# A decoder trunk on one core: combination tiles claimed early, gate chunks stored in pairs, the last three gate units kept on chip, weight units fetched a block ahead

## The chip, the cores and the metric

The kernel runs on one core of a Trainium2 chip. That core has a matrix engine (TensorE, PE in the profile, with a separate sequencer for the weight loads, PEld), a vector engine (VectorE, DVE), an activation engine (ScalarE, ACT), a general engine (GpSimd, POOL) and a queue engine (SyncE, SP), from which nearly all of this kernel's DMA transfers are issued. The metric is the device time of one execution, in microseconds; lower is better.

## The reference, cut to what matters

One layer of a decoder trunk is applied to 1024 prompt positions and to 8 samples of 4 new positions each, 1056 columns in all, at a model width of 1024. The middle part, which the change touches, is the mixing step between two feed-forward halves:

```
z = h @ w_in + b_in                         # q, k, v, uv, gate A, gate B
outs, lses = attention of 3 head groups (window, dilation) = (128,1), (512,4), (2048,16)
w   = softmax(lses over the 3 groups)       # one weight per head and position
att = sum over groups of outs * w           # "combination", 256 wide
yb  = u * (tril(W_s) @ LN(v) + b)           # gMLP branch, 512 wide
mix = (sigmoid(gA) * (att @ w_oa) + sigmoid(gB) * (yb @ w_ob)) @ w_out
h   = LN2(alpha * h + mix)
```

The prompt and the samples share all weights. The samples also attend to a cache of keys and values. Gate A and gate B are 1024 wide each, that is eight blocks of 128 rows each.

## The kernel before, in words

**Layout.** Activations lie transposed: 128 features on the partitions and 1056 columns (`NT`; the prompt alone is `NP` = 1024) along the free axis. The columns are worked in four chunks of `C` = 264. All products are in fp32r as three passes, high by high, high by low and low by high (`mm3`, L240), so that a weight and an activation are first split into a high and a low part (`split`, L251 on ACT and L252 on DVE).

**Pools.** `S` has 37 slots of a full row block (1056 columns), `W` 8 tiles for split weights, `M` 6 tiles of medium size, `R` and `Q` 2 each for raw data, and PSUM has 3 `mm` and 5 `ax` buffers. A tile takes the buffer of an older one when that one's last reader is done. `held` (L105 to L109) takes a slot and at once writes one column of it on POOL, so that the slot belongs to it from then on; without the write, the first real write claims it.

**Order of the work.** The program is written as generators in three queues (`bg`, `slow`, `mid`); `tick` steps them between two pieces of dense work. The Tile framework then schedules each engine's instructions by a simulated timeline, and a tag "urgent" draws an instruction forward. What an engine executes is therefore a fixed row of instructions, in the scheduler's order, and an engine waits at the first one that is not ready.

**The mixing stage.** `mix` (L1524) runs from about 1064 us to 1400 us of the profile.

- *Plain gate units.* Ten units (6 to 15 of the gate list, `NLEAD` = 6, `NTAIL` = 10) are dense products: one 128-wide block of `w_in` against eight blocks of `h`. `gate8` (L984 to L992) does one chunk: 24 matmuls into an `mm` buffer, an eviction on ACT into an `M` tile (L990), a store of the 132 KB chunk to the scratch array `zD` (L991), and a `tick`. Units 6 to 12 run all four chunks in the order 0, 2, 1, 3. Units 13 to 15 (`LAST` = 3) are fetched together and run chunks 0 to 2; their last chunk is run much later (`beside`), next to the output products.
- *Attention.* `attend(i)` runs six times, for the two head pairs and three groups (attend 0 to 2 are head pair 0, attend 3 to 5 head pair 1). Each has four steps of scores (L1200 on PE, bias and minimum L1208 on DVE, exponential L1212 on ACT), of turning the probabilities (L1223 on PE, copy L1227 on ACT) and of values (L1239 on PE, copy L1246 or L1250 on ACT), and at the end a transpose of the row minima and sums (L1261) that are stored to `mlD` (L1265). The dense chunks stand between the steps.
- *Combination.* After group 2 of a head pair, `combine(hp)` (L1272 to L1328) loads the minima and sums back (L1283 to L1289), computes the weights on DVE and ACT (L1297 to L1310), stores them to `cD` (L1312), fetches them broadcast over 64 partitions (L1319) and multiplies and adds on DVE (L1324, L1326, L1327). Its tiles are `raw`, `att` and three `cbs`; the last four are taken after the stores.
- *Samples.* The cached keys and values are loaded in pieces (`M<-kv`) and worked on DVE (L1392, L1397, L1398).
- *Output products.* `local(n)` multiplies gate B block n by `yb @ w_ob` (the product's eviction is the multiplication L1541 on DVE). The gate blocks `mt` are fetched from `zD` (L1138), and a narrow weight unit `wo` is fetched at the head of each block (`narrow`, L225 to L234). After the last `att` is split, the same is done for gate A (`ta`, fetched at L1580), block by block, with the late chunks of the units 13 to 15 beside blocks 2, 4 and 5. The sum of both is split for the last product, `w_out`.

## Time and profile before

| | us |
|---|---|
| median of 3 runs | 2202.6 (2198.51 to 2202.74) |
| profiled execution, device time | 2202.1 |
| its span in the trace | 2200.3 |
| busy in the span: PE, DVE, ACT, POOL | 2132.7, 1555.3, 892.8, 321.6 |
| mixing stage, 1064 to 1400 us: span and PE busy | 336.0 and 298.64 |

A row of the page names a line and engine, the operation, what it writes and reads by the program's names, how often it occurs, its total and mean time, and the idle time of that engine just before it with what ended the idle time. A timeline row has its start, its length, the engine, the line and operation, how many neighbouring instructions it sums up, and in brackets the idle time before it. In the windows table each engine has its busy time in that stretch and then the clock that PE was granted (1.00 is full).

### The profile page before, as it was taken

How to read it: one execution, taken by the hardware profiler on the slowest of the kernel's cores; microseconds unless marked ns; L12 is line 12 of the kernel's file. 1: busy time of each engine (PE TensorE's matmuls, PEld its weight loads, DVE VectorE, ACT ScalarE, POOL GpSimd, SP SyncE). 2: the span in 40 equal slices, each digit the busy share in tenths (PEclk: the TensorE clock that was granted, in tenths of full speed). 3: DMA queues.
4: the chain of work that ended last, by engine and by line, in shares of the span. 5: the costliest groups of instructions: out<-in, count | busy, mean ns of one | idle time of the engine just before them, and what ended most of it. 6: DMA issues, size and time to landing. Idle time of an engine off the chain costs nothing.

```text
span 2200.3 us, 43275 instructions
## 1 busy us (share of the span) xinstructions
PE 2132.7 (97%) x17305; PEld 2093.7 (95%) x17305; DVE 1555.3 (71%) x2724; ACT 892.8 (41%) x1681; POOL 321.6 (15%) x234
## 2 busy tenths in 40 slices
PE   9999999999998999999989988999999999999997
PEld 8999999999998999999879877999999999999997
DVE  8776776656788726787674647778576777656887
ACT  5444444421225634344465453245344444421224
POOL 0432332200010022232000000000332233100000
PEclk9999999999999999999999998999999999999998
DMA  4435545598973325666854637514354454597841
GB/s 157 146 134 178 176 161 175 194 372 319 329 279 134 136 101 193 205 219 222 312 166 151 186 119 244 195 41 143 129 185 156 166 185 159 181 393 290 303 183 79
DMA packets 170553, 429.01 MB, mean 195 GB/s; under 512 B 24864, under 2 KB 61584, under 8 KB 167664
## 3 DMA queue, kind: packets, MB, share of 16 engines
q1 hardware_dynamic: 169920, 425.71, 55.1%
q8 instruction: 135, 2.21, 0.4%
q14 instruction: 66, 0.54, 0.1%
q10 hardware_dynamic: 432, 0.54, 0.1%
HBM read 305.56 MB, written 166.81 MB: 215 GB/s over the span
## 4 chain that ended last, share of the span: by engine, by line
PE 83%; DMA 7%; DVE 6%; ACT 2%; issue 1%; SPq 1%; POOL 0%; ACTq 0%; DVEq 0%; POOLq 0%
PE ax L240 44%; PE mm L240 35%; DMA M<-kv 3%; DMA zD<-M 1%; DVE W L252 1%; PE ax L1200 1%; DMA S<-zD 1%; DVE X L1382 1%; PE ax L1223 1%; DVE S L252 1%; PE ax L1239 0%; DVE M L1392 0%; DVE S L627 0%; DVE M L1381 0%; DVE X L1397 0%
## 5 line engine op out<-in xcount | busy, mean ns | idle before, releaser
L240 PE MATMUL mm<-S,W 128*128 128x264 f32 x5208 | 694.8, 289 | 30.1 <-DVE S L1541 13.2
L240 PE MATMUL ax<-S,W 128*128 128x264 f32 x5400 | 706.9, 284 | 0.4 <-DVE W L252 0.2
L240 PEld LDWEIGHTS mm<-S,W 128*128 128x128 f32 x5208 | 659.2, 191 | 46.8 <-DVE S L1541 15.2
L240 PEld LDWEIGHTS ax<-S,W 128*128 128x128 f32 x5400 | 677.0, 188 | 2.7 <-ACT S L1030 0.8
L240 PE MATMUL ax<-S,S 128*128 128x264 f32 x3240 | 478.7, 285 | 4.0 <-DVE S L1039 3.9
L240 PEld LDWEIGHTS ax<-S,S 128*128 128x128 f32 x3240 | 429.6, 189 | 5.3 <-DVE S L1039 5.3
L240 PE MATMUL mm<-S,S 128*128 128x264 f32 x2472 | 383.8, 285 | 2.6 <-DVE S L252 2.0
L240 PEld LDWEIGHTS mm<-S,S 128*128 128x128 f32 x2472 | 333.7, 188 | 4.3 <-DVE S L252 2.2
L251 ACT CAST W<-R 128x1024 fp32r<-128x1024 f32 (+3 forms) x173 | 128.8, 761 | 319.7 <-PE mm L240 137.4
L382 POOL TENSOR_TENSOR Q<-R 128x512 f32<-128x512 f32 x49 | 70.3, 1434 | 798.2 <-DMA R<-w13a 202.8
L252 DVE TENSOR_TENSOR W<-R,W 128x1024 fp32r<-128x1024 f32 (+3 forms) x173 | 152.1, 883 | 26.7 <-ACT W L251 22.2
L251 ACT CAST W<-Q 128x1024 fp32r<-128x1024 f32 (+1 forms) x78 | 76.8, 984 | 224.2 <-POOL Q L383 89.4
L816 DVE SCALAR_TENSOR_TENSOR S<-ax,S 128x264 f32<-128x264 f32 x240 | 99.4, 427 | 66.8 <-PE ax L240 65.7
L457 DVE TENSOR_TENSOR S<-ax,M 128x264 f32<-128x264 f32 x82 | 32.8, 432 | 151.3 <-PE ax L240 151.3
L108 POOL CAST S<-ones 128x1 fp32r<-128x1 f32 x32 | 17.6, 571 | 751.4 <-DVE S L1633 363.5
L252 DVE TENSOR_TENSOR S<-Q,S 128x1024 fp32r<-128x1024 f32 (+1 forms) x78 | 112.6, 1444 | 3.8 <-ACT S L251 3.8
L252 DVE TENSOR_TENSOR W<-Q,W 128x1024 fp32r<-128x1024 f32 (+1 forms) x78 | 89.6, 1149 | 26.6 <-ACT W L251 26.6
L251 ACT CAST S<-Q 128x1024 fp32r<-128x1024 f32 (+1 forms) x78 | 76.8, 984 | 68.1 <-PE ax L240 49.7
L251 ACT CAST S<-R 128x512 fp32r<-128x512 f32 (+1 forms) x64 | 44.1, 689 | 105.9 <-DMA sumsA<-S 39.4
L252 DVE TENSOR_TENSOR S<-S,M 128x528 fp32r<-128x528 f32 x72 | 84.5, 1174 | 2.6 <-ACT M L251 0.8
L383 POOL TENSOR_TENSOR Q<-Q,R 128x512 f32<-128x512 f32 x49 | 81.0, 1653 | 2.7
L390 POOL TENSOR_TENSOR Q<-R,Q 128x512 f32<-128x512 f32 x49 | 80.5, 1644 | 1.1
(204 smaller groups left out, 2049.6 us busy)
## 6 DMA issues: line engine op xcount, KB each, us to landing
ws<-st SPq DMA_DIRECT2D x144, 256.0 KB
S<-sumsA SPq DMA_DIRECT2D x63, 528.0 KB
S<-sumsB SPq DMA_DIRECT2D x63, 528.0 KB
M<-kv SPq DMA_DIRECT2D x96, 256.0 KB
sumsA<-M SPq DMA_DIRECT2D x90, 264.0 KB
sumsB<-M SPq DMA_DIRECT2D x90, 264.0 KB
R<-w13b SPq DMA_DIRECT2D x44, 512.0 KB
R<-w13a SPq DMA_DIRECT2D x42, 512.0 KB
```

The lines of the kernel that those rows point to most:

```text
L108: self.nc.gpsimd.tensor_copy(t[:, 0, :1] if len(shape) == 3 else t[:, :1], self.ones[:, :1])
L240: mm = lambda a, b, s, e: nc.tensor.matmul(o, a[:, cc], b, start=s, stop=e, skip_group_check=True)
L251: a = self.nc.scalar.copy(hi, src)
L252: b = self.nc.vector.tensor_tensor(lo, src, hi.bitcast(F32), op=ALU.subtract)
L382: tt(s12[:, lo], cd[:, lo], cd[:, hi], op=ALU.add)
L383: tt(s12[:, hi], s12[:, lo], ab[:, lo], op=ALU.subtract)
L390: tt(s34[:, hi], ab[:, hi], s12[:, hi], op=ALU.subtract)
L457: go(one, 5, False, lambda x: tt(h[:, x, 1], one[x], p7[:, x], op=ALU.add))
L816: nc.vector.scalar_tensor_tensor(y(x, r, e), bank[x], HALF, y(x, r, e), op0=ALU.mult, op1=ALU.add)
L1200: nc.tensor.matmul(pS[h][:, r, :nk], q[e, i * P : (i + 1) * P], k[e, k0 : k0 + nk], start=True, stop=True)
L1223: nc.tensor.transpose(pT[r][:, h, o], s[:, r, h, o], self.ident)
L1382: nc.vector.tensor_reduce(o, t, axis=AX.X, op=ALU.add)
```

## The change

**Combination.** `combine` takes `raw`, `att` and the three `cbs` at its start, all five with `held`, so a one-column write on POOL claims each. Nothing else of its computation changes, but each `cb` is now a full-width slot of which `NP` columns are used.

**Plain gate units 6 to 12.** Each unit is fetched while the one before it is worked. The chunks 0 and 2 go into the two halves of one `W` tile, the chunks 1 and 3 into another (the last of these units uses `M` tiles), each pair with one store instead of two: 14 stores in place of 28.

**Units 13 to 15.** They are evicted straight into held slots (`kept`), chunk by chunk, and are neither stored to `zD` nor fetched back: 9 stores and 3 fetches go. The three units are fetched while unit 12 is worked, and the three slots are claimed then.

**Narrow units.** `wo` units are fetched one block ahead in both loops of output products.

Line numbers of the new program differ by a few from here on: L1585 is the eviction of a chunk pair, L1587 its store, L1569 the eviction of a kept unit, L1314 the store to `cD`.

```diff
@@ -1272,7 +1272,9 @@
     def combine(self, hp):
         nc = self.nc
         t = []
-        raw = self.S([16, 3, 2, P])
+        slot = self.held
+        raw = slot([P, 3 * 2 * P])[:16].rearrange("p (g m x) -> p g m x", g=3, m=2)
+        att, *cbs = [slot([P, NT]) for _ in range(4)]
         for g in range(3):
             x = raw[:, g]
             for m in range(2):
@@ -1311,15 +1313,13 @@
         for g in range(3):
             nc.sync.dma_start(self.cD[hp, g].rearrange("h (a x) -> (h a) x", a=8), t[g][:, 1])
         yield
-        att = self.S([P, NT])
         self.att[hp] = att
-        cbs = [self.S([P, NP]) for _ in range(3)]
         for g, cb in enumerate(cbs):
             for h in range(2):
-                nc.sync.dma_start(cb[64 * h : 64 * h + 64], self.cD[hp, g, h].partition_broadcast(64))
+                nc.sync.dma_start(cb[64 * h : 64 * h + 64, :NP], self.cD[hp, g, h].partition_broadcast(64))
         yield from self.pause(3)
         for g, cb in enumerate(cbs):
-            aT = self.attT.pop((hp, g))
+            cb, aT = cb[:, :NP], self.attT.pop((hp, g))
             if g == 0:
                 nc.vector.tensor_tensor(att[:, :NP], aT, cb, op=ALU.mult)
             else:
@@ -1541,7 +1541,9 @@
                 nc.vector.tensor_tensor(t[:, cc], t[:, cc], p, op=ALU.mult)
 
         def local(n):
-            wb = self.narrow(a["wo"][n, :, 2 * P :], 4 * P)
+            wb = wbs.popleft()
+            if n + 1 < KB:
+                wbs.append(self.narrow(a["wo"][n + 1, :, 2 * P :], 4 * P))
             if n + 6 < KB:
                 with self.tc.high_priority(offset=URGENT):
                     mt[n + 6] = self.fetch_z(40 + n)
@@ -1557,11 +1559,34 @@
         sgu = [self.sgu_norm()] + [self.sgu_mix(gg) for gg in range(4)]
         self.mid.extend(sgu)
         self.bg.extend(self.attend(i) for i in range(len(HPG)))
-        for n in range(NLEAD, NLEAD + NTAIL - LAST):
-            w = self.unit(a["wzp"][n])
-            for c in (0, 2, 1, 3):
-                self.gate8(w, DENSE[n], c, AF.Identity, STEPS["tail"], 1)
-        units = {n: self.unit(a["wzp"][n]) for n in range(NLEAD + NTAIL - LAST, NLEAD + NTAIL)}
+        kept, end = {}, NLEAD + NTAIL - LAST
+        units = {NLEAD: self.unit(a["wzp"][NLEAD])}
+
+        def gate(n, c, *steps):
+            p = self.mm_tile()[:, :C]
+            self.dense8(p, units[n], c)
+            with self.urgent():
+                nc.scalar.activation(kept[n][:, c * C : c * C + C], p, AF.Identity, bias=self.bin(DENSE[n]))
+            self.tick(*steps)
+
+        for n in range(NLEAD, end):
+            w = units.pop(n)
+            for m in range(n + 1, n + 2 if n + 1 < end else NLEAD + NTAIL):
+                units[m] = self.unit(a["wzp"][m])
+                if m >= end:
+                    kept[m] = self.held([P, NT])
+            z = self.zD[DENSE[n]].rearrange("p (a b x) -> p b a x", a=2, b=2)
+            for b in range(2):
+                t = (self.W if n + 1 < end else self.M)([P, 2, C], F32)
+                for x in range(2):
+                    p = self.mm_tile()[:, :C]
+                    self.dense8(p, w, 2 * x + b)
+                    with self.urgent():
+                        nc.scalar.activation(t[:, x], p, AF.Identity, bias=self.bin(DENSE[n]))
+                    if x:
+                        nc.sync.dma_start(z[:, b], t)
+                    self.tick(STEPS["tail"], 1)
+        w = None
         for c in range(NC):
             if c:
                 with self.tc.high_priority(offset=URGENT):
@@ -1569,23 +1594,9 @@
                         mt[n] = self.fetch_z(34 + n)
             if c < NC - 1:
                 for n in units:
-                    self.gate8(units[n], DENSE[n], c, AF.Identity, STEPS["tail"], 1)
+                    gate(n, c, STEPS["tail"], 1)
         while any(g in self.mid for g in sgu):
             self.step(self.mid, 1)
-
-        def fetch_gate(n):
-            held = 26 + n in [DENSE[m] for m in units]
-            t = self.S([P, NT])
-            cc = slice(0, (NC - 1) * C if held else NT)
-            nc.sync.dma_start(t[:, cc], self.zD[26 + n][:, cc])
-            return t
-
-        def beside(n):
-            m = DENSE[n] - 26
-            p = self.mm_tile()[:, :C]
-            self.dense8(p, units.pop(n), NC - 1)
-            with self.urgent():
-                nc.scalar.activation(ta[m][:, -C:], p, AF.Identity, bias=self.bin(DENSE[n]))
 
         def column_sums():
             wr, wsum = self.X([P, KB - half, KB], "wr", 1), self.X([P, KB], "wsum", 1)
@@ -1612,19 +1623,24 @@
         done, half = 0, 3
         sums = column_sums()
         self.slow.append(sums)
+        wbs = deque([self.narrow(a["wo"][0, :, 2 * P :], 4 * P)])
         for n in range(KB):
             local(n)
+        was = deque([self.narrow(a["wo"][0, :, : 2 * P], 2 * P)])
         self.yb = None
-        ta = [fetch_gate(n) for n in range(3)]
+        ta = [self.fetch_z(26 + n) for n in range(3)]
         while self.bg or self.mid or self.slow[0] is not sums:
             self.tick(1, 1 if self.slow[0] is not sums else 0)
         split_att()
 
         m2 = []
         for n in range(KB):
-            wa = self.narrow(a["wo"][n, :, : 2 * P], 2 * P)
+            wa = was.popleft()
+            if n + 1 < KB:
+                was.append(self.narrow(a["wo"][n + 1, :, : 2 * P], 2 * P))
             if n + 3 < KB:
-                ta.append(fetch_gate(n + 3))
+                m = NLEAD + NTAIL - KB + n + 3
+                ta.append(kept[m] if m in kept else self.fetch_z(29 + n))
             if 26 + n in LATE_GATES:
                 nc.scalar.activation(ta[n], ta[n], AF.Sigmoid)
             for c in range(NC):
@@ -1635,8 +1651,8 @@
             self.split(*m2[n], mt[n])
             done += 1
             if n in BESIDE:
-                beside(BESIDE[n])
-        units = self.A = None
+                gate(BESIDE[n], NC - 1, 0, 0)
+        units = kept = self.A = None
         self.sqs, self.lns = {}, {}
         self.Y = self.new_Y(self.hD[0])
 
```

How this moves the work on the engines is seen best at three places. Names have the letter of the pool and a number; `mm` and `ax` are PSUM buffers.

ScalarE around attend 3 (head pair 1, group 0), before: between the exponentials (L1212) and copies (L1227) of this attention stand evictions of gate chunks (L990).

```order
L990 ACTIVATE M_14702<-mm_14677,cols 128x264
L1212 ACTIVATE S_14316,X_14256<-S_14316,X_14256 128x256
L1212 ACTIVATE S_14316,X_14256<-S_14316,X_14256 128x256
L990 ACTIVATE M_14789<-mm_14764,cols 128x264
L1212 ACTIVATE S_14316,X_14256<-S_14316,X_14256 128x256 x2
L990 ACTIVATE M_14873<-mm_14848,cols 128x264
L1227 COPY S_14348<-ax_14339 128x512
L1227 COPY S_14348<-ax_14338 128x512
L990 ACTIVATE M_14913<-mm_14888,cols 128x264
L1212 ACTIVATE S_14351,X_14256<-S_14351,X_14256 128x256 x4
```

The same place of ScalarE after the change:

```order
L1227 COPY S_14338<-ax_14328 128x512
L1227 COPY S_14338<-ax_14329 128x512
L1212 ACTIVATE S_14341,X_14247<-S_14341,X_14247 128x256 x2
L1246 COPY S_14248<-ax_14321 128x512
L1212 ACTIVATE S_14341,X_14247<-S_14341,X_14247 128x256 x2
L1227 COPY S_14409<-ax_14399 128x512
L1227 COPY S_14409<-ax_14400 128x512
L1212 ACTIVATE S_14412,X_14247<-S_14412,X_14247 128x256 x4
L1227 COPY S_14476<-ax_14466 128x512
L1227 COPY S_14476<-ax_14467 128x512
L1569 ACTIVATE S_14498<-mm_14747,cols 128x264
L1569 ACTIVATE S_14507<-mm_14829,cols 128x264
```

The three first chunks of the kept units (`mm_14747`, `mm_14829`, `mm_14867`), whose matmuls stand on PE ahead of all of attend 3's turns, are evicted behind its last copies, each after its claim on POOL. There are three `mm` buffers, so no dense chunk stands on PE between these turns any more.

SyncE at the end of attend 5, before: the stores of the combination's weights and their fetches stand ahead of four fetches of gate blocks.

```order
L1312 DMA cD<-S_15274 16x128
L1312 DMA cD<-S_15274 16x128
L1319 DMA S_15307<-cD 64x1024
L1319 DMA S_15307<-cD 64x1024
L1319 DMA S_15308<-cD 64x1024
L1319 DMA S_15308<-cD 64x1024
L1319 DMA S_15309<-cD 64x1024
L1138 DMA S_15316<-zD_8666 128x1056
L1138 DMA S_15318<-zD_8667 128x1056
L1138 DMA S_15326<-zD_8668 128x1056
L1138 DMA S_15413<-zD_8669 128x1056
L1319 DMA S_15309<-cD 64x1024
```

The same four fetches of SyncE after the change, with the rows about them:

```order
L1138 DMA S_15118<-zD_8664 128x1056
L1138 DMA S_15120<-zD_8665 128x1056
L1285 DMA S_15239<-mlD 8x128
L1138 DMA S_15286<-zD_8666 128x1056
L1138 DMA S_15288<-zD_8667 128x1056
L1138 DMA S_15302<-zD_8668 128x1056
L1138 DMA S_15389<-zD_8669 128x1056
L1265 DMA mlD<-X_15200 32x128
L1285 DMA S_15239<-mlD 8x128
```

The fetches of `zD_8666` to `zD_8669` have moved ahead of the store of attend 5's minima and sums (L1265), and so ahead of the whole combination of head pair 1.

VectorE at the second combination, before: the multiplication L1324 stands ahead of four blocks of products (L1541 is the eviction of one chunk of a product).

```order
L1308 RECIPROCAL X_15287<-X_15287 16x128
L1310 TENSOR_TENSOR S_15274<-X_15287,S_15274 16x128 x3
L1324 TENSOR_TENSOR S_15306<-S_14257,S_15307 128x1024
L1326 TENSOR_TENSOR S_14630<-S_14630,S_15308 128x1024
L1434 COPY S_15306<-ax_15636 64x32 x2
L1541 TENSOR_TENSOR S_15316<-S_15316,mm_15622 128x264
```

The same place of VectorE after the change:

```order
L1312 TENSOR_TENSOR S_15239<-X_15261,S_15239 16x128 x3
L1607 TENSOR_REDUCE X_15618<-Q_15620 128x8
L1541 TENSOR_TENSOR S_15288<-S_15288,mm_15715 128x264
L252 TENSOR_TENSOR W_15730<-R_15729,W_15730 128x512
L1541 TENSOR_TENSOR S_15302<-S_15302,mm_15736 128x264
L1541 TENSOR_TENSOR S_15302<-S_15302,mm_15750 128x264
L1324 TENSOR_TENSOR S_15241<-S_14248,S_15243 128x1024
L1541 TENSOR_TENSOR S_15302<-S_15302,mm_15764 128x264
```

L1324 now has the products of the blocks fetched from `zD_8666` and `zD_8667` and half of the next ahead of it, and the rest between its own five instructions.

## The prediction, made before the changed kernel was run

> **What bounds the kernel now.** I read the page's span and busy times first, then its chain of waits, and then a windows table over the mixing stage, since the diff touches nothing outside it.
>
> ```profile
> span 2200.3 us, 43275 instructions
> PE 2132.7 (97%) x17305; PEld 2093.7 (95%) x17305; DVE 1555.3 (71%) x2724; ACT 892.8 (41%) x1681; POOL 321.6 (15%) x234
> PE 83%; DMA 7%; DVE 6%; ACT 2%; issue 1%; SPq 1%; POOL 0%; ACTq 0%; DVEq 0%; POOLq 0%
> ```
>
> PE is busy for 97% of the span and makes 83% of the chain, so time can only be had where PE stands or runs at a lower clock. The windows below cut the mixing stage at its joints; each row has the stretch, its length, busy times of PE, PEld, DVE, ACT and POOL, and PE's clock.
>
> ```profile
> 1064.00:1120.00 56.00, 51.38 (x418) 46.45 (x417) 28.78 (x84) 28.87 (x70) 0.00 (x0) 1.00 0.72 250
> 1120.00:1164.00 44.00, 34.73 (x261) 29.79 (x261) 34.00 (x89) 26.48 (x64) 0.00 (x0) 0.84 0.54 173
> 1164.00:1202.00 38.00, 38.00 (x317) 34.42 (x312) 18.10 (x62) 22.05 (x66) 0.00 (x0) 1.00 0.55 184
> 1202.00:1240.00 38.00, 35.86 (x293) 32.44 (x292) 26.11 (x59) 14.39 (x37) 0.00 (x0) 1.00 0.60 174
> 1240.00:1266.00 26.00, 24.18 (x208) 21.50 (x207) 13.55 (x53) 12.25 (x37) 0.00 (x0) 1.00 0.49 158
> 1266.00:1304.00 38.00, 34.71 (x312) 30.07 (x312) 16.63 (x74) 24.29 (x81) 0.00 (x0) 1.00 0.35 114
> 1304.00:1326.00 22.00, 12.28 (x102) 11.92 (x97) 12.98 (x38) 4.13 (x8) 0.00 (x0) 0.83 0.61 168
> 1326.00:1340.00 14.00, 12.99 (x86) 12.99 (x87) 11.75 (x20) 9.73 (x11) 0.00 (x0) 0.77 0.93 343
> 1340.00:1400.00 60.00, 54.52 (x428) 52.40 (x427) 48.11 (x78) 21.34 (x28) 1.38 (x3) 1.00 0.65 216
> sum 336.00, PE 298.64 PEld 271.98 DVE 210.01 ACT 163.55 POOL 1.38; mean PE 33.18 PEld 30.22 DVE 23.33 ACT 18.17 POOL 0.15
> ```
>
> PE stands 336.0 - 298.6 = 37.4 us, in lumps: 4.6 us at the start, 9.3 us in attend 0 and 1, nothing in attend 2, 2.1 + 1.8 = 4.0 us in attend 3, 3.3 us in attend 4 and 5, 10.7 us about 1326, 5.5 us after 1340. Three rows show a clock below 1. Their detail, in steps of 4 us:
>
> ```profile
> 1136.00:1140.00 4.00, 4.00 (x25) 2.69 (x24) 4.00 (x13) 2.48 (x8) 0.00 (x0) 0.50 0.84 288
> 1140.00:1144.00 4.00, 4.00 (x30) 3.83 (x29) 1.54 (x4) 1.05 (x5) 0.00 (x0) 0.85 0.99 330
> 1148.00:1152.00 4.00, 1.28 (x8) 0.93 (x8) 3.86 (x13) 1.86 (x8) 0.00 (x0) 0.93 0.40 118
> 1152.00:1156.00 4.00, 3.47 (x11) 2.59 (x12) 4.00 (x14) 2.62 (x6) 0.00 (x0) 0.50 0.45 133
> 1156.00:1160.00 4.00, 4.00 (x30) 3.86 (x30) 0.71 (x6) 2.64 (x11) 0.00 (x0) 0.72 0.51 169
> 1328.00:1332.00 4.00, 4.00 (x20) 4.00 (x19) 3.13 (x5) 2.63 (x3) 0.00 (x0) 0.50 1.03 335
> ```
>
> Busy time times the missing clock is lost on top of the idle time: 4.0 x 0.50 + 4.0 x 0.15 = 2.6 us after 1136, 3.47 x 0.50 + 4.0 x 0.28 = 2.8 us after 1152, and 2.0 us plus what precedes 1328, say 2.6 us, after the long idle spell. So 45 us in the mixing stage are there to be won, and the change can also add to them.
>
> **The change part by part.**
>
> *Stores, fetches, claims.* What ScalarE waited for stores (first row) and what a POOL claim takes (second):
>
> ```profile
> ACT M L990 <- DMA zD<-M: 20.3, 11, 3.4
> L108 POOL CAST S<-ones 128x1 fp32r<-128x1 f32 x32 | 17.6, 571 | 751.4 <-DVE S L1633 363.5
> ```
>
> Fourteen stores fewer by pairing, nine stores and three fetches fewer by keeping: 26 transfers less. The 20.3 us are waits of an engine that is busy 163.55 of 336 us, so I count nothing by themselves; what they release early is in the next term. The 13 new claims are 13 x 0.57 = 7.4 us on POOL, which has nothing else there before 1340: nothing either, unless a slot comes late (see attend 3). The new order puts two more table loads on ACT (one is shown below at 1.28 us): between 0 and 2.6 us, I take 0.5, as ACT has room.
>
> *Start, attend 0 and 1.* The lumps, as PE's and ACT's timelines show them:
>
> ```profile
> 1081.16 5.83 PE L240 MATMUL mm<-S,W 128*128 128x264 f32 x46 [2.96 <-ACT M L990]
> 1078.16 1.04 ACT L251 CAST W<-R 128x1024 fp32r<-128x1024 f32 x1 [10.14 <-issue]
> 1135.11 1.54 PE L1223 MATMUL ax<-ident,S 128*128 128x128 f32 x6 [5.88 <-ACT S L1212]
> 1152.16 2.73 PE L1200 MATMUL ax<-S,S 64*128 64x128 f32 x8 [1.21 <-DVE M L1519]
> 1304.15 9.09 PE L240 MATMUL mm<-S,W 128*128 128x264 f32 x72
> ```
>
> At 1081 PE waited 2.96 us because evictions stood behind a weight cast that ACT itself sat 10.14 us in front of. With units fetched ahead, three chunk evictions stand in front of that cast: -3.0 us. At 1135 PE waits for ACT's exponentials with its dense work used up; a dense matmul is 9.09 / 72 = 0.126 us. The new order has 85 dense matmuls between attend 0's last transpose and attend 1's first turn where 38 stood, 47 x 0.126 = 5.9 us more cover against 5.88 us. The last 13 of them need a fourth `mm` buffer while there are three, and so wait for an eviction behind the normalisation's activations: between nothing and 5.88 us stay, I take 2.7. In the rest of attend 1 (9.27 - 5.88 = 3.4 us idle) 112 dense matmuls stand where 47 stood, 8.2 us more; between 0 and 3.4 stay, I take 1.2 since the waits are short ones for DVE. The clock losses of 2.6 and 2.8 us follow from the idle time, and I keep 0.5 of them. Sum: 3.2 + 2.2 + 4.9 = -10.3 us, and with the start -13.3 us.
>
> Those matmuls are not new: by the end of attend 2 the new order has run 120 more (15.1 us), which are missing as cover later.
>
> *Attend 3, the loss.* The steps' durations, from a table of lines about attend 3:
>
> ```profile
> L1212 ACT ACTIVATE S<-S,X 128x256 f32<-128x256 f32 x10 | 5.0, 501 | 7.2 <-DVE X L1208 7.2
> L1208 DVE CUSTOM_DVE_ANT_0 S<-ax,M 128x256 f32<-128x256 f32 x10 | 3.9, 418 | 0.0
> 1242.97 1.09 PE L1223 MATMUL ax<-ident,S 128*128 128x128 f32 x8 [0.28 <-ACT S L1212]
> 1245.06 1.97 PE L240 MATMUL mm<-S,W 128*128 128x264 f32 x14
> 1246.96 1.09 PE L1239 MATMUL ax<-S,Q 128*64 128x128 f32 x16
> 1213.15 1.25 SPq L1312 DMA_DIRECT2D cD<-S  x3
> 1220.71 1.22 DVE L1324 TENSOR_TENSOR S<-S,S 128x1024 f32<-128x1024 f32 x1 [3.68 <-DMA S<-cD]
> ```
>
> Before, dense pieces (14 here) fill the steps and the whole attend costs 4.0 us of idle time. After, the first 72 kept matmuls stand ahead of all its turns, their evictions behind its last copies, and all three `mm` buffers are held: no dense work for some 25 us (below: 12 us of PE's attention work, four times 1.09 + 0.9 + 1.09, and 13 us of idle time). A bare step has 0.42 + 4 x 0.50 + about 0.3 = 2.7 us from the scores to the last exponential, of which the values (1.09 us) fill some: 1.6 us idle, four times, 6.4 us. DVE's L1324 of the first combination now stands ahead of the last scores' L1208. From the store of the weights to L1324 went 1220.71 - 1213.15 = 7.6 us, and DVE has one group of L1208 (4 x 0.42) and little else in between, so it stands up to 5.4 us there, and ACT, PE behind it. With 1.2 us for the samples' pieces that's 13 us, between 8 (little wait at L1324) and 25 (all of DVE's work in line). Idle +9.0 us. The clock falls in such a stretch as after 1152; I take +2.4 us, its lesser loss of the two sums above. Loss 11.4 us.
>
> The Trainium skill ("TensorE: Matmul & The Clock Gate", section "HAM oscillation — how this bites in real kernels") gives as a rule that PE needs no idle gaps above some 3.4 us to keep its clock. Here the trace differs: the row 1152:1156 has 0.50 after spells of at most 1.21 us, with PE busy 1.28 of the 4 us before. By the rule the 2.4 us would be nothing.
>
> *Attend 4 and 5.* The kept units' other chunks are spread more evenly; 3.3 us of idle time become 2.0, between 1 and 4: -1.3 us.
>
> *The end of the attention.* The long spell, as PE, DVE and SP show it:
>
> ```profile
> 1327.01 9.25 PE L240 MATMUL mm<-S,W 128*128 128x264 f32 x54 [10.73 <-DVE S L1541]
> 1321.90 1.23 DVE L1324 TENSOR_TENSOR S<-S,S 128x1024 f32<-128x1024 f32 x1 [6.17 <-DMA S<-cD]
> 1314.82 0.91 DVE L1310 TENSOR_TENSOR S<-X,S 16x128 f32<-16x128 f32 x3
> 1319.91 2.00 SPq L1138 DMA_DIRECT2D S<-zD  x4
> 1326.17 1.28 ACT L1549 ACT_TABLE_LOAD   x1
> ```
>
> DVE stood at L1324 for the broadcast weights with the products' evictions (L1541) behind it, and even these needed gate blocks that SP could only ask for at 1319.91. After the change the four fetches stand ahead of the combination on SP, and L1324 behind ten of the L1541 that it held up. The 10.73 us and the 2.6 us of clock go. What is late next: from L1324's place the chain L1324, two L1326, two L1327 and the split (six at about 1.23 us, 7.4 us, with the L1541 and a wait of some 4 us between, 18 us from L1310) against nine products of 12 matmuls, 9 x 1.5 = 13.6 us: some 5 us of PE idle ahead of the first gate A product. Net -8.3 us. From both sides: DVE is busy 12.98 + 11.75 + 48.11 = 72.8 of the 96 us after 1304 and PE 79.8, so at best the stage ends 16 us earlier; at worst the 10.73 us come back ahead of gate A, which gives nothing. The two narrow fetches ahead serve parts of the 5.5 us after 1340, which I leave.
>
> *Sum.* -3.0 - 10.3 + 11.4 - 1.3 - 8.3 + 0.5 = -11.0 us against the profiled execution's 2202.1 us, which is 0.5 us below the median of the three runs: 2191 us.
>
> **The rivals.**
>
> *Slower: DVE in line in attend 3.* The bare stretch may cost far more. The piece-wise work for the samples (L1392 and L1397, each taken at the 0.67 us of the first row below, six pairs, 8 us) shares DVE with L1208 there, its loads have made DVE wait before, and L1324 adds 5.4 us:
>
> ```profile
> L1392 DVE TENSOR_TENSOR M<-M,X 128x512 f32<-128x512 f32 x8 | 5.2, 673 | 3.0 <-DMA M<-kv 3.0
> DVE M L1392 <- DMA M<-kv: 14.9, 6, 8.0
> ```
>
> With 6.4 + 8 + 5.4 us and one wait of 8.0 us, 27.8 us instead of 4.0, and PE's 12 us of attention work at half clock (6 us), the loss is 30 us: 2202.1 - 22.4 + 30 = 2210 us. It decides from a loss in attend 3 above 22.4 us on, which is what all other terms win. Against it: part of these pieces ran earlier. Also the third kept slot is that of a probability tile of attend 3 itself, so the evictions can't come sooner than I took them.
>
> *The end gives nothing.* DVE, at 48.11 of 60 us in the last row, becomes the bound and the idle spell moves to the gate A products: 2191 + 8.3 = 2199 us.
>
> *The first part does not work.* If PE's waits in attend 0 and 1 are the attention's own chain and not missing dense work, only the start is won there: 2191 + 10.3 = 2201 us. Against it: attend 2, with the same chain and dense work, has no idle time at all.
>
> *The clock holds in attend 3.* If it falls only after long spells, as after those of 5.88 and 10.73 us, and attend 3's are of some 2 us each, its 2.4 us don't come: 2191 - 2.4 = 2189 us; the row of 1152 speaks against it. This is what the rule on the page of the Trainium skill named above, "TensorE: Matmul & The Clock Gate", amounts to here.
>
> **How the numbers follow.** My forecast 0.54 (its own range 2181 to 2198), slower by DVE 0.24, the end 0.10, the first part 0.07, the clock 0.05. No change means within 0.2%, 4.4 us, which is about what a measurement of this kernel can tell. Below that are the forecast and the clock, and the edge of the end: 0.60. Within it the end, the first part, and the near edge of the slow case: 0.17. Slower: 0.23. The range goes from 2180, where the end gives twice its 8.3 us, to 2210, the slow rival.
>
> **What would show it.** Right: PE's wait of 5.88 us for L1212 and the clock below 1 about 1136 gone; attend 2's end about 13 us earlier; then a stretch of 25 to 30 us in attend 3 with PE busy for half of it and clock rows near 0.5; no wait of 10 us for L1541. Wrong: an attend 3 stretch beyond 35 us, DVE's waits for `M<-kv` or `S<-cD` above 10 us in it, or a new spell of PE in front of the gate A products longer than 8 us.

## The result and the profile after

The changed kernel takes 2192.3 us in the median of 5 runs (2190.17 to 2195.08); the kernel before took 2202.6 us in 5 runs beside it (2198.51 to 2204.14). The ratio is 0.996, with a 95% interval of 0.9946 to 0.9974. The forecast was 2191 us. The change made the kernel faster by 0.4%; single parts of the forecast were off by more than their sum, since their errors cancel, as follows.

The head of the page of the changed kernel:

```profile
span 2190.5 us, 43256 instructions
PE 2133.8 (97%) x17305; PEld 2092.5 (96%) x17305; DVE 1548.1 (71%) x2724; ACT 894.4 (41%) x1683; POOL 327.1 (15%) x247
```

PE does the same 17305 instructions; the span is 9.8 us shorter. Where that comes from is seen best at marks that both kernels pass. The table counts from the end of the last product of the stage before; the marks are the starts of L1261, PE's last transpose of an attend (rows of the timeline), and the first product of the statistics behind the mixing. "Dense" is the number of dense matmuls that stand on PE in that part by the order of instructions, and "beyond" is the part's time less 0.126 us for each of them: what the attention, waits and a lower clock take. The other rows are those of the experiments below.

| kernel | to attend 2's end: us, dense, beyond | attend 3: us, dense, beyond | attend 4 and 5: us, dense, beyond | rest, us | all, us |
|---|---|---|---|---|---|
| before | 133.3, 513, 68.7 | 54.5, 293, 17.6 | 50.1, 208, 23.9 | 122.9 | 360.8 |
| after | 132.1, 639, 51.6 | 40.8, 105, 27.6 | 57.3, 276, 22.6 | 118.6 | 348.9 |
| only_combination | 136.6, 513, 72.0 | 52.2, 284, 16.4 | 49.7, 217, 22.4 | 117.3 | 355.9 |
| only_pairs | 131.5, 639, 51.0 | 55.2, 177, 32.8 | 49.2, 204, 23.5 | 121.8 | 357.7 |
| only_kept | 134.4, 513, 69.7 | 50.5, 225, 22.2 | 53.4, 219, 25.8 | 122.7 | 361.1 |
| only_narrow | 134.6, 513, 70.0 | 53.6, 293, 16.7 | 49.1, 208, 22.9 | 123.5 | 360.8 |
| weights_later | 131.3, 639, 50.8 | 37.2, 105, 23.9 | 57.4, 276, 22.6 | 118.8 | 344.6 |
| chunks_in_turns | 132.8, 639, 52.2 | 56.6, 105, 43.3 | 54.1, 260, 21.3 | 120.2 | 363.5 |
| without_kept | 133.0, 639, 52.5 | 47.5, 177, 25.2 | 49.2, 204, 23.5 | 118.1 | 347.8 |
| adds_on_pool | 131.3, 639, 50.8 | 40.9, 105, 27.7 | 57.2, 276, 22.5 | 122.2 | 351.6 |
| later_and_without_kept | 133.2, 639, 52.7 | 47.4, 177, 25.1 | 49.4, 204, 23.7 | 120.3 | 350.3 |
| less_vector_work | 131.6, 633, 51.8 | 39.5, 111, 25.5 | 53.1, 253, 21.3 | 121.8 | 346.0 |
| without_sums | 132.1, 639, 51.6 | 42.6, 105, 29.3 | 58.1, 276, 23.3 | 118.1 | 350.9 |
| without_combination | 132.5, 639, 52.0 | 54.6, 105, 41.4 | 53.9, 259, 21.3 | 123.4 | 364.4 |

Each row of the table is one profiled execution, and parts that run the same instructions in the same order on every engine show its spread. Up to attend 2's end this holds for the kernel before, only_combination, only_kept and only_narrow, with 68.7 to 72.0 us beyond; in attend 3 it holds for the changed kernel, adds_on_pool and without_sums, with 27.6 to 29.3 us. Differences of 2 to 3 us in one part are thus not taken for effects by themselves.

So the whole change gains 68.7 - 51.6 = 17.1 us up to attend 2, loses 27.6 - 17.6 = 10.0 us in attend 3, gains 1.3 us in attend 4 and 5, and 4.3 us at the end, of which 0.8 us are six dense matmuls that had already run. That is 11.9 us in the mixing stage. The spans differ by 2 us less, since PE came to the stage 2.2 us later in this profile. That is spread: in weights_later and without_sums, whose rows of instructions are the changed kernel's up to there, it came at 1064.81 and 1068.76 us, here at 1067.16 us.

The early part, in windows of the changed kernel (columns as before):

```profile
1084.00:1120.00 36.00, 36.00 (x306) 31.69 (x306) 19.32 (x60) 22.51 (x56) 0.00 (x0) 1.00 0.51 177
1120.00:1136.00 16.00, 13.76 (x100) 13.05 (x99) 14.51 (x33) 12.99 (x26) 0.00 (x0) 0.89 0.53 174
1136.00:1164.00 28.00, 28.00 (x248) 25.54 (x247) 19.26 (x54) 15.26 (x43) 0.00 (x0) 1.00 0.61 194
```

PE stands 2.24 us in all up to attend 2's end, where it stood 13.9 us, and only one of these rows has a clock below 1. The whole 2.24 us is the fourth chunk that waits for an `mm` buffer, as foreseen:

```profile
1129.36 4.72 PE L240 MATMUL mm<-S,W 128*128 128x264 f32 x24 [2.24 <-ACT W L1585]
```

Attend 3, as PE's timeline and DVE's show it:

```profile
1199.30 0.27 PE L1261 MATMUL ax<-ident,X 128*32 128x128 f32 x1
1204.04 10.91 PE L240 MATMUL mm<-S,W 128*128 128x264 f32 x88
1218.19 0.55 PE L1223 MATMUL ax<-ident,S 128*128 128x128 f32 x3 [3.24 <-ACT S L1212]
1224.57 0.66 PE L1223 MATMUL ax<-ident,S 128*128 128x128 f32 x4 [1.66 <-ACT S L1212]
1238.34 1.97 PE L1223 MATMUL ax<-ident,S 128*128 128x128 f32 x8 [4.47 <-ACT S L1212]
1240.10 0.42 PE L1261 MATMUL ax<-ident,X 128*32 128x128 f32 x1
```

```profile
1200.29 1.33 DVE L1392 TENSOR_TENSOR M<-M,X 128x512 f32<-128x512 f32 x2 [2.57 <-DMA M<-kv]
1208.26 0.22 DVE L1299 COPY X<-S 16x128 f32<-16x128 f32 x1 [3.42 <-DMA S<-mlD]
1216.84 0.27 DVE L1208 CUSTOM_DVE_ANT_0 S<-ax,M 128x128 f32<-128x128 f32 x1
1235.59 1.23 DVE L1324 TENSOR_TENSOR S<-S,S 128x1024 f32<-128x1024 f32 x1 [5.70 <-DMA S<-cD]
```

The DVE spell of 5.70 us at L1324 is the one that was forecast at up to 5.4 us; PE's 4.47 us behind it are its price. The first PE spell, 3.24 us, had only 1.2 us for the samples' pieces in the forecast: PE had written the scores by 1204, and DVE came to them only at 1216.84. At the end of the attention PE's waits have become many and short:

```profile
PE mm L240 <- DVE S L1541: 9.9, 11, 2.0
```

### The profile page after: what moved, and what is told of

It reads as the page before. It is cut to its first block, busy times and chain, and to the rows that moved or that the text cites. A ratio compares the mean times of both kernels' runs of the same rounds, so it can differ in the third digit from the quotient of the medians.

```text
span 2190.5 us, 43256 instructions
## 1 busy us (share of the span) xinstructions
PE 2133.8 (97%) x17305; PEld 2092.5 (96%) x17305; DVE 1548.1 (71%) x2724; ACT 894.4 (41%) x1683; POOL 327.1 (15%) x247
## 5 line engine op out<-in xcount | busy, mean ns | idle before, releaser
L240 PEld LDWEIGHTS mm<-S,W 128*128 128x128 f32 x5208 | 657.8, 190 | 39.6 <-DVE S L1541 11.4
L251 ACT CAST W<-R 128x1024 fp32r<-128x1024 f32 (+3 forms) x173 | 128.6, 761 | 306.9 <-PE mm L240 155.3
L382 POOL TENSOR_TENSOR Q<-R 128x512 f32<-128x512 f32 x49 | 68.7, 1403 | 797.6 <-DMA R<-w13a 183.9
L251 ACT CAST W<-Q 128x1024 fp32r<-128x1024 f32 (+1 forms) x78 | 76.7, 984 | 221.3 <-POOL Q L383 88.9
L252 DVE TENSOR_TENSOR W<-Q,W 128x1024 fp32r<-128x1024 f32 (+1 forms) x78 | 89.7, 1150 | 27.8 <-ACT W L251 27.6
L251 ACT CAST S<-Q 128x1024 fp32r<-128x1024 f32 (+1 forms) x78 | 76.8, 984 | 69.2 <-PE ax L240 50.2
L251 ACT CAST S<-R 128x512 fp32r<-128x512 f32 (+1 forms) x64 | 44.0, 688 | 105.8 <-DMA sumsA<-S 39.1
```

The lines of the kernel that those rows point to most:

```text
L240: mm = lambda a, b, s, e: nc.tensor.matmul(o, a[:, cc], b, start=s, stop=e, skip_group_check=True)
L251: a = self.nc.scalar.copy(hi, src)
L252: b = self.nc.vector.tensor_tensor(lo, src, hi.bitcast(F32), op=ALU.subtract)
L382: tt(s12[:, lo], cd[:, lo], cd[:, hi], op=ALU.add)
```

## The experiments

**Each part alone.** Four kernels put one part of the change into the kernel before.

The combination's claims alone:

```diff
-        raw = self.S([16, 3, 2, P])
+        slot = self.held
+        raw = slot([P, 3 * 2 * P])[:16].rearrange("p (g m x) -> p g m x", g=3, m=2)
+        att, *cbs = [slot([P, NT]) for _ in range(4)]
...
-        att = self.S([P, NT])
-        cbs = [self.S([P, NP]) for _ in range(3)]
```

> The kernel before with the combination's five claims alone. If these claims are what moves L1324 behind the products' evictions at the end of attend 5 (theory): the stretch from attend 5's last transpose to the last gate A product, 94.7 us before and 90.4 us after the whole change, comes down to some 90 to 91 us, nothing changes up to attend 5, and the time is 2198 to 2199 us. If the narrow units fetched ahead or the three fetches saved give that gain (rival): 94 to 95 us in that stretch and 2202 to 2203 us.

Measured: 2198.0 us, ratio 0.9973 (0.9957 to 0.9988). This is the theory's value. The rest after attend 5 falls by 5.6 us. PE's longest wait for L1541 in that kernel's end, and its longest wait there, for ScalarE's part of a split (L251), are

```profile
1335.54 3.97 PE L240 MATMUL mm<-S,W 128*128 128x264 f32 x18 [2.10 <-DVE S L1541]
1343.78 1.03 PE L240 MATMUL mm<-S,W 128*128 128x264 f32 x3 [3.11 <-ACT S L251]
```

where 10.73 us stood. The claims alone give the end's gain.

The pairs and the units fetched ahead alone:

```diff
-        for n in range(NLEAD, NLEAD + NTAIL - LAST):
-            w = self.unit(a["wzp"][n])
-            for c in (0, 2, 1, 3):
-                self.gate8(w, DENSE[n], c, AF.Identity, STEPS["tail"], 1)
+        for n in range(NLEAD, end):
+            w = units.pop(n)
+            for m in range(n + 1, n + 2 if n + 1 < end else NLEAD + NTAIL):
+                units[m] = self.unit(a["wzp"][m])
...
+                    if x:
+                        nc.sync.dma_start(z[:, b], t)
```

> The kernel before with the stores of two chunks and the units 6 to 15 fetched a unit ahead; the units 13 to 15 are stored and fetched as before, the combination and the narrow units are as before. Theory (the early part comes from here, the loss in attend 3 from the kept units' evictions): attend 2 ends at about 1199 us with 126 more dense matmuls done, attend 3 costs at most 3 us more idle time than before, no gain at the end, 2190 us. Rival (the loss comes from having run the dense work early, kept or not): the same early part, then attend 3 without dense work for 20 us and more, a loss of 8 to 9 us there, 2195 us.

Measured: 2199.3 us, ratio 0.9981 (0.9967 to 0.9996), slower than both expectations. All of the early gain is there (beyond 51.0 us), no gain at the end, and attend 3 loses 15.2 us although no unit is kept, more than the 8 to 9 us of the rival. Its longest waits for the exponentials on PE in that kernel, beside two spells of 2.22 and 1.82 us for an `M` tile, are:

```profile
1227.98 0.55 PE L1223 MATMUL ax<-ident,S 128*128 128x128 f32 x3 [0.71 <-ACT S L1212]
1240.76 1.12 PE L1223 MATMUL ax<-ident,S 128*128 128x128 f32 x4 [9.31 <-ACT S L1212]
```

That the kept units' evictions make attend 3 long is thereby ruled out as the main cause.

The kept slots alone (units fetched as before):

```diff
-                    self.gate8(units[n], DENSE[n], c, AF.Identity, STEPS["tail"], 1)
+                    gate(n, c, STEPS["tail"], 1)
...
+            kept[m] = self.held([P, NT])
```

> The kernel before with the units 13 to 15 evicted into kept slots alone (9 stores and 3 fetches fewer). Theory (these evictions make attend 3 bare): no gain up to attend 2, 8 to 9 us lost in attend 3 and the beginning of attend 4, 2210 us. Rival (running ahead makes it bare): within 2 us of before, 2201 to 2204 us.

Measured: 2202.2 us, ratio 0.9995 (0.9985 to 1.0006): no change, as the rival had it. 4.6 us beyond are lost in attend 3 and 1.9 us in attend 4 and 5. The end wins as much: it takes in the 57 dense matmuls (7.2 us) that these parts no longer run, and is no longer than before. Nothing of the twelve transfers shows in the time.

The narrow units alone:

```diff
-            wb = self.narrow(a["wo"][n, :, 2 * P :], 4 * P)
+            wb = wbs.popleft()
+            if n + 1 < KB:
+                wbs.append(self.narrow(a["wo"][n + 1, :, 2 * P :], 4 * P))
```

> The kernel before with the narrow units of the output products fetched a block ahead alone. Theory: their fetches were mostly hidden; 2201 to 2203 us, the spell of 10.7 us before L1541 stays. Rival (the end's gain is theirs): the spell shrinks and the time is 2198 us.

Measured: 2202.6 us, ratio 0.9995 (0.9983 to 1.0007): no change, the spell before L1541 still 10.9 us, as the theory had it.

By the medians the parts alone add up to some 8 us and by the ratios to some 12 us, where the whole gives 10 and 9; with some 3 us of uncertainty in a ratio, these sums don't show whether the parts work on each other. The marks do: only_pairs has the early part of the whole change, but loses 15.2 us in attend 3 where the whole loses 10.0. The next runs ask why.

**Without the combination's claims.** The changed kernel with the function `combine` of before.

> The changed kernel with the combination as before (its tiles taken late, no claims). If the claims alone move L1324 at the end, the stand of some 6 us at L1324 and PE's spell of 10 us before L1541 come back, and the stretch after attend 5 is 3 to 5 us longer: 2195 to 2198 us. If the kept units or the narrow units do it too: 2191 to 2193 us.

Measured: 2206.4 us, ratio to before 1.0022 (1.0013 to 1.0032). Neither expectation holds: the claims are worth 14 us within the change. The end is 4.8 us longer, as the first had it; attend 3 is 13.8 us longer, with the same 105 dense matmuls. DVE, then PE, of this kernel:

```profile
1209.17 0.22 DVE L1297 COPY X<-S 16x128 f32<-16x128 f32 x1 [4.48 <-DMA S<-mlD]
1214.46 0.69 DVE L1392 TENSOR_TENSOR M<-M,X 128x512 f32<-128x512 f32 x1 [4.17 <-DMA M<-kv]
1228.90 0.28 DVE L1208 CUSTOM_DVE_ANT_0 S<-ax,M 128x128 f32<-128x128 f32 x1
```

```profile
1204.46 10.91 PE L240 MATMUL mm<-S,W 128*128 128x264 f32 x88
1230.27 0.90 PE L1223 MATMUL ax<-ident,S 128*128 128x128 f32 x3 [14.90 <-ACT S L1212]
1242.96 1.12 PE L1223 MATMUL ax<-ident,S 128*128 128x128 f32 x4 [7.72 <-ACT S L1212]
```

PE is as early as in the changed kernel. What differs is DVE's row: here all of the combination's arithmetic (L1297 to L1310) and the samples' pieces up to it stand ahead of the first L1208 of attend 3, and L1324 behind the first four. In the changed kernel the first L1208 stand amid that arithmetic, at 1216.84 instead of 1228.90, and L1324 behind the first twelve. Up to that first L1208 the two kernels have the same order on DVE, and PE's order is the same through all of attend 3. Of the 12 us, some 3 are later loads (the L1392 shown at 1214.46 starts at 1211.07 in the changed kernel), the rest is the order. The only_pairs kernel, without claims too, has its first L1208 at 1226.61. So the claims do two things by moving the combination on DVE: at the end of attend 5 and in attend 3.

**Chunks among the turns.** The first chunks of the kept units were held behind attend 3's turns.

```diff
+                if c == 0:
+                    key = (1, 0, n - end)
+                    while key not in self.turns:
+                        self.step(self.bg, 1)
+                    ctx.enter_context(self.tc.issue_after(self.turns[key]))
                 self.dense8(p, units[n], c)
```

> The changed kernel with the first chunks of the three kept units issued behind the first, second and third turn of attend 3, so that 72 dense matmuls stand among its turns and not ahead of them. Theory of the prediction (these turns are long because dense work is missing in them): 8 to 10 us of idle time and 2.5 us of clock go, 2182 to 2185 us. Rival (attend 3 goes at the pace of DVE's row of work and its loads, and dense work only moves the idle time about): PE stands some 9 us ahead of attend 3's first turn instead, and the time stays within 2 us of the changed kernel's, 2190 to 2194 us.

Measured: 2206.2 us, ratio to before 1.0015 (1.0003 to 1.0026). Neither expectation holds. PE and DVE of this kernel:

```profile
1205.03 2.20 PE L241 MATMUL mm<-S,W 128*128 128x264 f32 x16
1229.58 0.90 PE L1224 MATMUL ax<-ident,S 128*128 128x128 f32 x3 [22.35 <-ACT S L1213]
```

```profile
1228.16 0.29 DVE L1209 CUSTOM_DVE_ANT_0 S<-ax,M 128x128 f32<-128x128 f32 x1 [0.31 <-DMA cD<-S]
```

The dense work went among the turns and PE stood ahead of them for 22.35 us. 9 us of that are the 72 matmuls held back; the rest is that DVE's row moved as well, its first scores (L1209 here) to 1228.16 behind the combination, so the run is no clean test of the dense work alone. From its first turn to its last transpose attend 3 takes 27.3 us here with 9.1 us of dense work, 21.9 us in the changed kernel without. By that, cover among the turns would be worth some 3.7 us, not the 10 us that the theory wanted. How much a held chunk would give with DVE's row unchanged stays open.

**L1324 later.** In the changed kernel, one more order is set: L1324 of the first combination behind the last L1208 of attend 3.

```diff
+            if g == 0 and not hp:
+                while (1, 0) not in self.scored:
+                    yield
+                with self.tc.issue_after(self.scored[1, 0]):
+                    nc.vector.tensor_tensor(att[:, :NP], aT, cb, op=ALU.mult)
```

> The changed kernel with one order more: the first combination's L1324 is issued behind attend 3's last L1208 instead of ahead of that group. Theory (DVE's stand of 5.7 us at L1324 sets the end of attend 3): PE's wait of 4.5 us for the exponentials goes, attend 3 ends 5 to 6 us earlier, 2186 to 2188 us. Rival (the stretch is long for want of dense work, and DVE's stand only fills time that another wait would take): attend 3 within 2 us of its length, 2190 to 2193 us.

Measured: 2184.6 us (2183.73 to 2187.1), ratio to before 0.9924 (0.9909 to 0.9938), whose interval lies below that of the changed kernel. On every engine its order is the changed kernel's up to the place where L1324 stood. The first and the last turn of attend 3 in this kernel, and L1324 (here L1330):

```profile
1216.82 0.90 PE L1226 MATMUL ax<-ident,S 128*128 128x128 f32 x3 [5.03 <-ACT S L1213]
1232.05 1.42 PE L1226 MATMUL ax<-ident,S 128*128 128x128 f32 x8 [0.32 <-ACT S L1213]
1233.56 1.23 DVE L1330 TENSOR_TENSOR S<-S,S 128x1024 f32<-128x1024 f32 x1 [2.10 <-DMA S<-cD]
```

PE's 4.47 us are 0.32 us. From its first turn to its last transpose attend 3 takes 16.5 us instead of 21.9, which is the theory's 5 to 6 us. By the marks it is 3.6 us shorter, between the two expectations, since PE stood 5.03 us ahead of the first turn in this profile and 3.24 us in the other, where the order is the same. The stage is 4.3 us shorter. The medians differ by 7.6 us, more than the theory had; of the difference between the two profiles 2.4 us lie ahead of the stage, where nothing was changed, and are spread. It's the fastest kernel of this study.

**Without kept slots.** The changed kernel with units 13 to 15 through `gate8`, `fetch_gate` and `beside` as before.

> The changed kernel with the units 13 to 15 stored and fetched as before (9 stores and 3 fetches more), everything else kept. If the kept units' evictions cost attend 3 its cover, attend 3 ends 5 us and more earlier and the time is 2186 us or less. If not, and the saved transfers and even spread are worth something, it is slower than the changed kernel: 2193 to 2197 us.

Measured: 2188.3 us (2184.48 to 2191.64), ratio to before 0.9938 (0.9919 to 0.9957). That lies between the two expectations. It is 4.0 us under the changed kernel, but the intervals overlap and the stages differ by 1.1 us: no gain of the kept slots is seen, and they may cost a little. Attend 3 is 2.4 us shorter beyond its dense work, far from the 5 us and more and little above the spread.

**Both.** The two edits together.

> The changed kernel with both earlier edits: the first combination's L1324 behind attend 3's last L1208, and the units 13 to 15 stored and fetched as before. The first was worth 7.6 us, the second 4.0 us. If attend 3 goes at the pace of VectorE's row of work, the DVE stand of 5.9 us that the second still had goes as well and the gains add up in the main: 2181 to 2184 us. If both gains come out of the same idle time: 2184 to 2188 us.

Measured: 2192.0 us, ratio to before 0.994 (0.9926 to 0.9955): slower than both expectations, with no gain over either edit. The edit orders only L1324. In this build the scheduler drew the two other multiplications (L1326, here L1334) to its old place, ahead of the last four L1208, and PE waits as before:

```profile
DVE S L1334 <- DMA S<-cD: 5.2, 2, 4.1
1244.15 1.97 PE L1226 MATMUL ax<-ident,S 128*128 128x128 f32 x8 [6.64 <-ACT S L1213]
```

The stand moved from one instruction of the combination to another, still ahead of the last scores, and attend 3 takes 47.4 us against 47.5 us without the order.

**Less work for VectorE in attend 3.** The multiplications of the third sample pair are left out.

```diff
-            nc.vector.tensor_tensor(t, t, p.unsqueeze(1).to_broadcast(t.shape), op=ALU.mult)
+            if ip != 2:
+                nc.vector.tensor_tensor(t, t, p.unsqueeze(1).to_broadcast(t.shape), op=ALU.mult)
```

> The changed kernel without the 17 multiplications L1392 of the third sample pair (0.67 us each, some ten of them on VectorE around attend 3); this part of the samples' attention is left out of the computation, PE's order in attend 3 stays the same. If attend 3 goes at the pace of VectorE's row, PE's first turn there comes 3 to 6 us earlier and attend 3 ends 4 to 7 us earlier (2184 to 2188 us). If the loads (keys and values, minima and sums) set its pace, VectorE waits longer for them instead, and attend 3 ends within 2 us of the changed kernel's.

Measured: 2187.9 us, ratio to before 0.9929 (0.9915 to 0.9942), below the changed kernel's interval and in the range of the first expectation. But attend 3 ends only 1.3 us earlier by the marks, 2.1 us beyond its dense work, as the second had it. PE's first turn comes 22.6 us after attend 2's mark instead of 18.9, after a spell of 6.22 us. DVE waits for the samples' loads in place of working on them. Over the mixing stage, of this kernel (its L1398 is the sum L1397 of the changed one) and then of the changed one:

```profile
DVE X L1398 <- DMA M<-kv: 11.1, 6, 4.2
```

```profile
DVE M L1392 <- DMA M<-kv: 5.7, 6, 2.6
```

So ahead of the first turn it is not the amount of DVE's work that sets the pace, but the loads for which DVE stands in its row with the scores behind them. From the first turn on attend 3 takes 16.9 us instead of 21.9. The scheduler's order is another one in this kernel, though, on DVE from 1153 us of the changed kernel on, and PE runs six dense matmuls more in attend 3, so that this run does not separate the amount of work from its order there.

**The end: column sums left out, and additions on GpSimd.**

```diff
-                nc.vector.tensor_reduce(
-                    wr[:, q], raw.rearrange("p (k x) -> p k x", x=P), axis=AX.X, op=ALU.add
-                )
+                nc.vector.tensor_copy(wr[:, q], raw[:, :KB])
```

> The changed kernel with the five column sums of the last weight (L1607, 1.21 us each on VectorE between 1323 and 1360 us) replaced by short copies; the sums are thereby left out of the computation. If VectorE's amount of work bounds the output products, the stretch after attend 5 becomes 4 to 6 us shorter (2186 to 2188 us). If it is the wait of 3 us at L1324, ScalarE's casts and the chain to the first gate A product that bound it: less than 2 us (2190 to 2192 us).

Measured: 2193.8 us, ratio to before 0.9951 (0.9931 to 0.997); the rest after attend 5 is 118.1 us against 118.6 us. 6 us less work on DVE give 0.5 us there, as the second expectation had it: the amount of work isn't the bound. That the kernel is no faster in all lies in attend 3, 1.8 us longer in this profile by the spread.

```diff
-            nc.vector.tensor_tensor(mt[n], mt[n], ta[n], op=ALU.add)
+            (nc.gpsimd if n < KB - 1 else nc.vector).tensor_tensor(mt[n], mt[n], ta[n], op=ALU.add)
```

> The changed kernel with seven of the eight additions of the gated products (L1649, 1.25 us each on VectorE) on GpSimd. If VectorE bounds the output products at the end (it is busy 53.7 of the 60 us from 1320 to 1380), 8.75 us of its work go and the end becomes 3 to 6 us shorter: 2187 to 2189 us. If its waits for loads and for ScalarE bound it, or if GpSimd is slow enough to delay the splits: 2191 to 2196 us.

Measured: 2195.8 us, ratio to before 0.9978 (0.9968 to 0.9987); the rest is 3.6 us longer, as the second expectation had it. The same splits of DVE in 1338 to 1378 us, of the changed kernel and then of this one:

```profile
L252 DVE TENSOR_TENSOR S<-S,S 128x1056 fp32r<-128x1056 f32 x6 | 7.5, 1251 | 0.2 <-ACT S L251 0.2
```

```profile
L252 DVE TENSOR_TENSOR S<-S,S 128x1056 fp32r<-128x1056 f32 x6 | 11.5, 1915 | 0.9 <-ACT S L251 0.9
```

Most of what GpSimd took from VectorE it gave back in longer splits: VectorE is busy 67.8 of the 88 us from 1300 to 1388 us instead of 69.3, though 8.75 us of additions are gone. More of this in the last section.

## Why the prediction was right, point by point

The change of time came as forecast, by a gain early, a loss in attend 3 and a gain at the end. That the sum came within 1.3 us of the measured median is luck in part: the early gain was forecast 3.8 us too small and the end's 4.0 us too large, and attend 3 has two errors that cancel as well.

- *Stores, fetches, claims at nothing* held for the transfers (only_kept and only_narrow: no change). For the claims it was wrong in kind: they cost nothing on POOL, but in the whole change they are worth 14 us through DVE's row, of which the prediction saw the end only. The 0.5 us for two more table loads on ACT were measured by no run.
- *Start, attend 0 and 1*, -13.3 us: measured -17.1 us. The idle time fell from 13.9 to 2.24 us, to less than the 5.5 us that I let stand; of the clock's 5.4 us some 1.5 stayed (13.76 us busy at 0.89). The mechanism, dense work ready a unit earlier, is that of the forecast; only_pairs has all of it alone. The cover between attend 0's last transpose and attend 1's first turn was 102 dense matmuls where 55 stood, 17 more on both sides than the prediction counted, so its difference of 47 holds. What I kept back for short waits in attend 1 and at the start was too much.
- *Attend 3*, +11.4 us: measured +10.0 us. The stretch without dense work ran from 1214.95 to 1240.10 us, 25 us as forecast. L1324's stand (5.4 us forecast, 5.70 us measured) with its effect was shown by weights_later. The rest of the size is luck: PE's idle time rose from 3.9 to 10.4 us, by 6.5 and not 9.0 us, as the bare steps cost 2.7 us together where I had 6.4, and the clock took more than forecast (next point). The cause that I put first, the kept units' evictions, is not the main one: only_pairs, which keeps no unit, loses 15.2 us there; only_kept loses 4.6 us, and within the change the kept units cost some 2.4 us (without_kept), little above the spread. The length is mainly set by where DVE's combination and the samples' waits for loads stand ahead of the scores: without_combination makes it 13.8 us longer with the same order on PE. That the want of dense work lets PE feel it is argued from the order; chunks_in_turns gives some 3.7 us for it among the turns, but moved DVE's row too.
- *The clock there*, +2.4 us: the forecast called this the lesser of its two sums, but these are 2.6 and 2.8 us. In the rows of the changed kernel below, busy time times the missing clock is 3.4 us in all. Ahead of the rows of 0.69 to 0.88 PE stood for no more than 3.24 us at a time. The row of 0.50 has the spell of 4.47 us. So the rival in which the clock holds fell; it took all spells there for some 2 us, though the forecast itself had PE behind a stand of up to 5.4 us.

```profile
1216.00:1220.00 4.00, 1.81 (x9) 1.47 (x11) 3.44 (x15) 2.38 (x9) 0.00 (x0) 0.84 0.73 222
1220.00:1224.00 4.00, 2.88 (x19) 1.24 (x17) 3.85 (x12) 1.54 (x5) 0.00 (x0) 0.73 0.48 154
1224.00:1228.00 4.00, 3.39 (x16) 2.09 (x16) 4.00 (x13) 1.94 (x8) 0.00 (x0) 0.69 0.34 97
1228.00:1232.00 4.00, 3.53 (x32) 2.72 (x32) 1.89 (x11) 3.31 (x11) 0.30 (x2) 0.88 0.31 88
1232.00:1236.00 4.00, 1.36 (x18) 0.83 (x16) 0.41 (x1) 1.07 (x2) 0.19 (x2) 0.97 1.05 253
1236.00:1240.00 4.00, 1.66 (x8) 1.66 (x9) 3.62 (x11) 2.16 (x9) 0.00 (x0) 0.50 0.61 132
```

- *Attend 4 and 5*, -1.3 us: measured -1.3 us. That it is the same number is luck: PE's idle time there went from 2.9 us to nothing, and a row at 0.67 behind attend 3's last spell took 1.3 us of it back.
- *The end*, -8.3 us: measured -4.3 us, or -3.5 us beyond the dense work. This is the term that was mis-sized. The spell of 10.73 us went as said, and its cause, the place of L1324, is shown by only_combination and without_combination. But from attend 5's mark on PE still stands 12.0 us, where it stood 16.7 us, and 9.9 us of that are eleven short waits for L1541. Without the long spell 5.9 us would have been left; I had 5 us more, and 6.1 us came. The clock's 2.6 us did not all go either: behind one of these waits, of 2.04 us, stands the row below, which loses 1.7 us. The rest of the difference shows in PE's busy time and stays open. The rival had DVE's amount of work for it; without_sums speaks against that. What remains, the chain from L1324 and the casts on ScalarE, was not tested.

```profile
1348.00:1352.00 4.00, 4.00 (x22) 4.00 (x22) 3.98 (x7) 1.38 (x2) 0.00 (x0) 0.57 0.64 213
```

- The rival in which attend 3 makes the kernel slower is not what happened, but it was near: without_combination and chunks_in_turns are that case, at 2206 us, through DVE's row as the rival had it.

## What to carry to other kernels

Where a scheduler fixes each engine's row, fetching ahead makes dense work ready early, and it is used up early; what stands later with less cover then shows the waits that the cover had hidden. Before one spreads the cover again, look at the engine that feeds the bare stretch: one instruction that waits for a transfer, ahead of work that is ready, cost 4 to 5 us here (weights_later), and a whole row of small ones ahead of that work cost 14 us (without_combination). A single order that put the one behind made the fastest kernel of this study.

## What the runs showed of the hardware

GpSimd's additions slowed VectorE's splits by the time that both overlap. DVE, then POOL, of adds_on_pool:

```profile
1344.79 0.43 DVE L1541 TENSOR_TENSOR S<-S,mm 128x264 f32<-128x264 f32 x1 [0.89 <-PE mm L240]
1349.22 3.56 DVE L252 TENSOR_TENSOR S<-S,S 128x1056 fp32r<-128x1056 f32 x1
```

```profile
1344.04 2.46 POOL L1649 TENSOR_TENSOR S<-S,S 128x1056 f32<-128x1056 f32 x1 [2.73 <-DVE S L1541]
1349.18 2.48 POOL L1649 TENSOR_TENSOR S<-S,S 128x1056 f32<-128x1056 f32 x1 [2.69 <-DVE S L1541]
```

The split began 0.04 us after the second addition and took 3.56 us instead of 1.25, which is 2.3 us more, about the addition's 2.48 us. L1541, which has one input in PSUM, took its usual 0.43 us beside the first. The Trainium skill ("SBUF — State Buffer", section "SBUF: two separate sides") says that VectorE and GpSimd share one pair of ports that one instruction holds for its whole length, also against a VectorE instruction with two SBUF inputs; these rows agree.
